# Output projection by tile groups with kept weight tiles, operand sums on VectorE, and one pool for merge and MLP

## The chip, the cores and the metric

The kernel runs on one core of a Trainium2 chip. The metric is the device time of one execution in microseconds. Before the change it is 1648.05 us, the median of three runs (1645.05, 1648.05 and 1648.10 us).

## The reference, cut to what matters

One layer of a decoder: two attention branches on the same normalized input, a gated merge, an output projection, and an MLP with squared ReLU. T = 1024 rows, D = 1024, DFF = 4096, everything in fp32. The change lies behind the attention branches, from `merged` on.

```python
def rms_norm(x, g):
    return x * rsqrt(mean(x * x, axis=-1) + 1e-6) * g

# o_fox, o_nsa [T, 512]: outputs of the attention branches; g_a, g_b [T, D]: columns of h @ w_in
merged = sigmoid(g_a) * (o_fox @ w_br_fox) + sigmoid(g_b) * (o_nsa @ w_br_nsa)
x = x + merged @ w_out                          # w_out [1024, 1024]
h = rms_norm(x, g_mlp)
x = x + square(relu(h @ w_ff1)) @ w_ff2         # w_ff1 [1024, 4096], w_ff2 [4096, 1024]
return rms_norm(x, g_final)
```

## The kernel before

**A product in fp32.** An operand is split into a high part, its cast to float32r ("hi", on ScalarE), and a low part, the operand less its high part ("lo", a subtraction). A product is three TensorE passes: lo x hi, hi x lo, hi x hi. All matmuls are issued on L157 and all transposes on L160, so the tile names tell them apart. A weight of the output projection is loaded into a buffer `wr` (2 of them), cast to `wh` (L205) and subtracted to `wl` (L206, VectorE); there are 3 buffers of each. The queue of a `w` load is SP's, as that of nearly all loads and stores; SP issues them in program order, and one that waits for a buffer holds those behind it.

**What is behind the attention.** `merge` computes the second branch product and keeps `merged`, transposed and split (its low part on L1394, VectorE), as `mrg[half] = (mh, ml)`, a half being 512 rows, that is four row tiles of 128. Then four pieces follow.

1. *w_out.* Its 1024 x 1024 weights are taken in eight blocks of 256 rows by 512 columns, 512 KB each. A block (u, ch) times a row tile i is six matmuls of 128 x 512, "a tile" below, accumulated in a psum bank `wo`. There are three groups: row tiles 0 to 3 (`wout0`, 2 x 16 tiles), row tiles 4 and 5, row tiles 6 and 7 (`wout1`, 16 tiles each). Every group loads and splits all eight blocks, 24 in all. When a row tile's column half is complete, `x1_done` adds the residual (L1441), and after the second half stores the row tile to DRAM (L1443), works out the RMS factor (L278 and L265 are small operations of it) and scales by it and by g_mlp (L1449).
2. *Turning.* The MLP needs h transposed. `turned` issues four 128 x 128 transposes into one of two psum banks (`psT`, tiles `tn_m`): "a turn". `first_half` (row tiles 0 to 3) casts it to hi (L1498, ScalarE), subtracts to lo (L1499, VectorE) and copies it to `bf` (L1506, ScalarE). `second_half` (row tiles 4 to 7) forms the sums that the scheme of the MLP needs, t1 to t4 (L1515, L1522, L1524 on VectorE or ScalarE, L1526 and L1529 on POOL), and splits each; two of the splits, and those of `rest`, go to POOL through the argument `eng`.
3. *w_ff1.* It is one level of a seven-product Strassen-Winograd scheme (`FIRST`), with operand sums on both sides. The 4096 columns are taken in 16 pairs u of two 128-column halves; `raw_half(u, x)` loads one half (512 KB, `r4`, four buffers), `wsum` forms the pair's weight sums on POOL (L1616 to L1619), `wsplit1` casts and splits the operands of one of four groups g (L1606, L1607; `w1h`, `w1l`). A product i of a pair is `ff1(u, i)`: three passes of four matmuls into bank X, W or Z. Products 0 and 1 need no sums. For three leading pairs (`LEADU`) they are issued ahead of the rest, between the last turns. `ff1_done` reads the banks, squares and stores hidden tiles to DRAM (`hid_d`); for the leading pairs this is put off (`defer`) until the pool `ff` opens in `hidden`, which does the rest of the scheme.
4. *w_ff2* in `output`: a second scheme of seven products, its weights loaded in quadrants of 8 KB per partition (pools `fo` and `f0`) and subtracted to their low parts on L1777 (VectorE, tiles `to`), and the final norm.

**What sets the order.** Python issues the instructions; the Tile scheduler orders them per engine by its estimates, dependences and the pools' buffers. `tc.issue_after(self.last.ins)` pins a TensorE step behind the one before. `placed(at, extra, steps)` puts the extra steps (the turns) at the places `at` among the numbered steps: a turn at 6.1 stands behind step 6. The tables `FFT1` and `FFT` are these places in the third group and among the leading products; the turns of the second group were spread evenly by `interleave`. A pool opened later than another gets its memory when the tiles there are released.

Of the kernel before, what the change touches and what calls it, by code (L numbers as in the profile page):

```python
# [18 lines left out]
P = 128  # L19
T = 1024  # L20
D = 1024
NT = 8
# [102 lines left out]
class Kernel:  # L125
# [1247 lines left out]
    def merge(self):  # L1373
# [6 lines left out]
        with tc.tile_pool(name="x1", bufs=8) as xp, tc.tile_pool(name="mg", bufs=3) as mp:  # L1380
            self.att = mp
            box = {}
            mrg = [None, None]
            st = Steps()

            def done(f, half, ps, sg):
                sg, pf = sg
                nc.vector.tensor_mul(sg, ps, sg)
                nc.vector.tensor_add(sg, sg, pf)
                if mrg[half] is None:  # L1390
                    mrg[half] = (hx_tile(f"mh{half}") if half else self.big_tile("mh0"), hx_tile(f"ml{half}"))
                th, tl = (t[:, f] for t in mrg[half])
                nc.scalar.copy(th, sg)
                nc.vector.tensor_sub(tl, sg, th.bitcast(F32))  # L1394

            def stage(f, half):

                if f < 2:
                    if not box:
                        box["t"] = self.big_tile("msn", F32)  # L1400
                    c = 4 * f + 2 * half
                    t = box["t"][:, c:c + 2]
                else:
                    t = xp.tile([P, 2, H], F32, tag="o", name=f"msn{f}{half}")
                for x, d in enumerate((self.gb_d, self.ga_d)):
                    nc.sync.dma_start(t[:, x], d[f * P:(f + 1) * P, half * H:(half + 1) * H])
                return t[:, 0], t[:, 1]

            self.branch(st, a["w_br_nsa"], stage, "n", lambda: self.on, done, True)
            self.commit(st)  # L1410
            wo = {}

            def wo_add(r, ch, u):
                wo[r, ch, u] = self.wadd([(None, a["w_out"][u * 256:u * 256 + 256, ch * H:ch * H + H].rearrange(
                    "(k p) c -> p k c", p=P))], f"wo{r}{ch}{u}", shape=(2, H), now=True)
# [21 lines left out]
            def x1_done(i, ch, acc):
                x = x1[i]
                th, j = divmod(i, 4)
                c = slice(ch * H, ch * H + H)  # L1440
                nc.vector.tensor_add(x[:, c], acc, x[:, c])  # L1441
                if ch == 1:
                    nc.sync.dma_start(self.x1_d[i * P:(i + 1) * P, :], x)  # L1443

                    junk = dest("t1" if th else "b11", j, self.big_tile, whole=True)
                    r = self.rstd(x.rearrange("p (a b) -> p a b", b=P), junk, f"m{i}")
                    for c in range(2):
                        cs = slice(c * H, c * H + H)
                        nc.vector.scalar_tensor_tensor(x[:, cs], x[:, cs], r, gm[:, cs], OP.mult, OP.mult)  # L1449
                    ys[th].append([x[:, 0:H], x[:, H:D]])  # L1450

            def wout0(ch):
                acc = [(self.psS if j < 2 else self.psP)(f"wo0{ch}{j}") for j in range(4)]

                def part(u, j):
                    wpart(acc[j], mrg[0], wo[0, ch, u], 2 * u, slice(j * P, j * P + P), u == 0, u == 3)
                    if u == 3:
                        x1_done(j, ch, acc[j])

                return [(6 * MM, lambda u=u, j=j: part(u, j)) for u in range(4) for j in range(4)]  # L1460

            def wout1(r):
                acc = {(ch, j): (self.psP if ch else self.psS)(f"wo1{r}{ch}{j}") for ch in range(2) for j in range(2)}

                def part(u, ch, j):
                    i = 2 * (r - 1) + j
                    wpart(acc[ch, j], mrg[1], wo[r, ch, u], 2 * u, slice(i * P, i * P + P), u == 0, u == 3)
                    if u == 3:
                        x1_done(4 + i, ch, acc[ch, j])

                return [(6 * MM, lambda u=u, ch=ch, j=j: part(u, ch, j))
                        for u in range(4) for ch in range(2) for j in range(2)]

            gm = mp.tile([P, D], F32, tag="gm", bufs=1, name="g_mlp_b")
            nc.sync.dma_start(gm, ap(a["g_mlp"], 0, [[0, P], [1, D]]))
            for i in range(NT):
                xt = xp.tile([P, D], F32, tag="o", name=f"x1_{i}")
                nc.sync.dma_start(xt, a["x"][i * P:(i + 1) * P, :])
                x1.append(xt)


            V = self.hv = {}

            def turned(y, c, name):
                pt = self.psT(f"tn_{name}_{c}")
                for k in range(4):
                    self.tr(pt[:, k * P:(k + 1) * P], y[c][:, k * P:(k + 1) * P], self.idn)
                return pt.rearrange("p (k t) -> p k t", k=4)

            def dest(key, j, alloc, whole=False):  # L1490
                if key not in V:
                    V[key] = alloc(f"h{key}")
                t = V[key][:, :, j * P:(j + 1) * P]
                return t if whole else (t[:, 0:4], t[:, 4:8])

            def split(key, j, src, alloc, eng, full=None):
                hi, lo = dest(key, j, alloc)
                nc.scalar.copy(hi, src)  # L1498
                eng.tensor_sub(lo, src if full is None else full, hi.bitcast(F32))  # L1499

            def first_half(j, c):
                pv = turned(ys[0][j], c, f"m0{j}")
                split("b21" if c else "b11", j, pv, self.big_tile, nc.vector)
                if c == 0:
                    bf.append(xp.tile([P, 8, P], F32, tag="o", name=f"bf{j}"))
                nc.scalar.copy(bf[j][:, 4 * c:4 * c + 4, :], pv)  # L1506
# [55 lines left out]
            for f in rest:  # L1562
                f()
# [388 lines left out]
```

## Time and profile before

| | |
|---|---|
| median of three runs | 1648.05 us |
| profiled execution, its own time | 1649.16 us |
| its span (first to last instruction) | 1647.5 us |
| granted TensorE clock, mean over the span | 0.984 |
| busy, share of the span | PE 97%, PE's weight load 82%, VectorE (DVE) 67%, ScalarE (ACT) 52%, GpSimd (POOL) 25% |
| DMA queues | 37.7% of 16 engines' span |

In the rows below, PE is a matmul or transpose, PEld its weight load, L157 a line of the kernel. A row of the list of groups gives line, engine, operation, output<-inputs, shapes and count, then the busy time and the mean in ns of one, then the engine's idle time just ahead of them and what ended it. A row of the list of waits gives the waiting group, what released it, the total in us, the count and the longest. A row of the chain gives when a piece began and how long it was. A row of stretches has the window in us from the span's start, its length, the busy time of PE, PEld, DVE, ACT and POOL, each with its count, then the granted clock (1.00 is full speed), the share of the DMA engines and GB/s.

### The profile page before, as it was taken

Reading aid. Unit: us, or ns where it says so; the run is one execution under the profiler, and the core shown is the slowest. Engines: PE = TensorE matmul, PEld = TensorE weight load, DVE = VectorE, ACT = ScalarE, POOL = GpSimd, SP = SyncE. Lnnn points to the kernel's source line nnn. Section 1 sums busy time; section 2 is a strip of 40 time slices with the busy share of each in tenths; the row PEclk is TensorE's granted clock in tenths of the full one; section 3 lists DMA queues with packets and bytes.
Section 4 is the critical chain, followed back from the end, with each engine's and each line's share of the span. In section 5 each row is a group of like instructions: output and inputs, shape, how many; then the busy total and the mean of one; then the engine's idle time right before and its main releaser. Section 6 shows DMA issues by size and latency. Waiting matters only on the chain.

```text
span 1647.5 us, 23820 instructions
## 1 busy us (share of the span) xinstructions
PE 1596.6 (97%) x8245; PEld 1351.1 (82%) x8245; DVE 1102.1 (67%) x2339; ACT 861.2 (52%) x1636; POOL 416.6 (25%) x486
## 2 busy tenths in 40 slices
PE   6999999999999999999999998799999999999997
PEld 5788888888888888898988876688888878888886
DVE  8556666765655675576767479565566579787876
ACT  4456566645555565567553265555555544333334
POOL 7122122212333322346330007433333200000004
PEclk7999999999999999999999998899999999999999
DMA  5321211342222212124348561454444597444412
GB/s 171 59 68 35 60 61 35 111 113 62 69 56 64 65 38 73 53 65 140 126 150 273 196 216 63 148 175 144 157 146 152 183 326 245 150 136 155 135 52 102
DMA packets 166080, 198.79 MB, mean 121 GB/s; under 512 B 21112, under 2 KB 100792, under 8 KB 165952
## 3 DMA queue, kind: packets, MB, share of 16 engines
q1 hardware_dynamic: 165960, 197.27, 37.7%
q8 instruction: 65, 1.06, 0.3%
q14 instruction: 55, 0.45, 0.1%
HBM read 142.09 MB, written 55.15 MB: 120 GB/s over the span
## 4 chain that ended last, share of the span: by engine, by line
PE 86%; DVE 6%; DMA 4%; issue 2%; ACT 2%; POOL 1%; SPq 0%; ACTq 0%; DVEq 0%; POOLq 0%
PE g L157 11%; PE fX L157 10%; PE accs L157 8%; PE oX L157 8%; PE fZ L157 5%; PE oZ L157 4%; PE ptn L160 4%; PE fq L157 3%; PE nq L157 3%; PE fv L157 3%; PE brf L157 3%; PE wo L157 3%; PE fk L157 3%; PE sf L157 2%; PE brn L157 2%; PE fW L157 2%
## 5 line engine op out<-in xcount | busy, mean ns | idle before, releaser
L157 PE MATMUL oX<-to,so 128*128 128x512 f32 x672 | 155.3, 390 | 1.9 <-DVE to L1777 1.3
L157 PEld LDWEIGHTS oX<-to,so 128*128 128x128 f32 x672 | 125.9, 188 | 29.2 <-DVE to L1777 1.7
L1776 ACT CAST to<-w 128x1024 fp32r<-128x1024 f32 x48 | 48.1, 1051 | 143.9 <-PE accs L157 53.2
L820 DVE TENSOR_TENSOR PTn<-ptn,PTn 128x512 fp32r<-128x512 f32 (+2 forms) x136 | 82.0, 610 | 52.0 <-ACT PTn L819 51.4
L819 ACT CAST PTn<-ptn 128x512 fp32r<-128x512 f32 (+2 forms) x136 | 69.3, 521 | 55.5 <-PE ptn L160 49.4
L1892 POOL TENSOR_TENSOR z<-x,gf 128x512 f32<-128x512 f32 x14 | 18.9, 1369 | 310.9 <-DVE x L1825 307.5
L157 PE MATMUL fX<-ht,w1h 128*128 128x512 f32 x384 | 95.8, 392 | 0.0
L796 POOL TENSOR_SCALAR pf<-pf,rdf 128x896 f32<-128x896 f32 (+3 forms) x64 | 47.4, 748 | 178.7 <-DVE rdf L795 154.0
L157 PE MATMUL accs<-PTn,Vnv 128*128 128x256 f32 x480 | 91.0, 305 | 0.0
L157 PEld LDWEIGHTS fX<-ht,w1h 128*128 128x128 f32 x384 | 72.9, 190 | 15.4
L1607 DVE TENSOR_TENSOR w1l<-w,w1h 128x1024 fp32r<-128x1024 f32 (+1 forms) x32 | 37.6, 1174 | 65.4 <-ACT w1h L1606 65.3
L157 PE MATMUL g<-hTl,wh_g 128*128 128x512 f32 (+1 forms) x280 | 78.0, 399 | 0.0
L157 PE MATMUL oZ<-to,so 128*128 128x512 f32 x336 | 77.5, 389 | 0.0
L157 PEld LDWEIGHTS accs<-PTn,Vnv 128*128 128x128 f32 x480 | 72.2, 189 | 2.7 <-DVE otn L829 0.4
L157 PEld LDWEIGHTS oZ<-to,so 128*128 128x128 f32 x336 | 63.1, 188 | 13.1
L157 PE MATMUL g<-hTh,wh_g 128*128 128x512 f32 (+1 forms) x280 | 73.2, 389 | 0.0
L157 PE MATMUL g<-hTh,wl_g 128*128 128x512 f32 x256 | 72.2, 400 | 0.0
L1777 DVE TENSOR_TENSOR so<-hr,so 128x1024 fp32r<-128x1024 f32 x56 | 68.3, 1240 | 2.6 <-ACT so L1776 2.5
L1776 ACT CAST so<-hr 128x1024 fp32r<-128x1024 f32 x56 | 56.5, 1049 | 17.7 <-DMA hr<-hid_d 17.7
L1616 POOL TENSOR_TENSOR ss<-w 128x512 f32<-128x512 f32 x16 | 26.2, 1639 | 144.6 <-DVE w1l L1607 136.8
L1777 DVE TENSOR_TENSOR to<-w,to 128x1024 fp32r<-128x1024 f32 x48 | 56.7, 1223 | 7.7 <-ACT to L1776 7.7
L157 PE MATMUL fX<-ht,w1l 128*128 128x512 f32 x192 | 52.4, 395 | 9.5 <-ACT h L1680 8.8
(521 smaller groups left out, 4393.8 us busy)
## 6 DMA issues: line engine op xcount, KB each, us to landing
hr<-hid_d SPq DMA_DIRECT2D x56, 512.0 KB, 4.9
w<-in_w_ff_dram SPq DMA_DIRECT2D x32, 512.0 KB, 4.6
hid_d<-s SPq DMA_DIRECT2D x64, 256.0 KB, 2.0
w<-in_w_ff_dram SPq DMA_DIRECT2D x15, 1024.0 KB, 5.7
wr_wo<-in_w_out_dram SPq DMA_DIRECT2D x24, 512.0 KB, 4.5
hid_d<-h SPq DMA_DIRECT2D x48, 256.0 KB, 2.9
x<-in_x_dram SPq DMA_DIRECT2D x16, 512.0 KB, 7.1
wr_g<-in_w_in_dram SPq DMA_DIRECT2D x16, 512.0 KB, 3.9
```

Source lines behind the costliest of these rows:

```text
L157: self.last = self.nc.tensor.matmul(*a, **k)
L160: self.last = self.nc.tensor.transpose(*a, **k)
L796: nc.gpsimd.tensor_scalar(p, p, r, 1.0 if gate is None else gate, op0=OP.mult, op1=OP.mult)
L819: nc.scalar.copy(th, src)
L820: nc.vector.tensor_sub(tl, src, th.bitcast(F32))
L1607: nc.vector.tensor_sub(lo, src, hi.bitcast(F32))
L1616: e.tensor_add(p[:, 4:8], b[:, 0:4], b[:, 4:8])
L1776: nc.scalar.copy(o[:, 0, s], src)
L1777: nc.vector.tensor_sub(o[:, 1, s], src, o[:, 0, s].bitcast(F32))
L1892: nc.gpsimd.tensor_mul(y[:, c], x[:, c], gf[:, c])
```

## The change

- w_out goes by the row tile groups (0, 1, 4, 5), (2, 3) and (6, 7). Inside a group the order of blocks is written out (`WO`) so that the first two blocks of the second and third group are the last two of the group before: their split tiles are kept (`wo[r, u, ch] = wo[r - 1, u, ch]`) and not loaded again. 20 blocks are loaded.
- Row tiles 0, 1, 4, 5 are done first, so turns of both halves stand in the second group (table `AT1`, one turn after each of six tiles), and first-half turns of tiles 2 and 3 in the third (`AT2`).
- All sums and splits of `second_half` and `rest` are on VectorE, and `wsum` of pair 0 too; t3 and t4 are formed in place.
- One pool `o4` of 4 KB tiles (8 under tag "o", 2 under tag "p") serves x1, the buffers of the turns, the hidden tiles of w_ff1 and the weights of w_ff2, which are therefore loaded in half quadrants. The pools `x1`, `mg`, `ff`, `f0` and `fo` are gone; the leading pairs' `ff1_done` follow straight behind the leading products.
- There are four leading pairs. The fourth pair's first half is loaded behind the last turn of `AT3`; its banks are `psT`, which the turns have left.

```diff
-        with tc.tile_pool(name="x1", bufs=8) as xp, tc.tile_pool(name="mg", bufs=3) as mp:
+        xp = self.o4 = self.ctx.enter_context(tc.tile_pool(name="o4", bufs=8))
...
-            for ch in range(2):
-                for u in range(4):
-                    wo_add(0, ch, u)
-            for r in (1, 2):
-                for u in range(4):
-                    for ch in range(2):
-                        wo_add(r, ch, u)
+        for r, blocks in enumerate(self.WO):
+            for n, (u, ch) in enumerate(blocks):
+                if r and n < 2:
+                    wo[r, u, ch] = wo[r - 1, u, ch]
+                    continue
+                wo[r, u, ch] = self.wadd(...)
...
+        gm = xp.tile([P, D], F32, tag="p", bufs=2, name="g_mlp_b")
+        odd = xp.tile([P, 2, H], F32, tag="p", bufs=2, name="odd")
...
-            def split(key, j, src, alloc, eng, full=None):
+        def split(key, j, src, alloc):
                 hi, lo = dest(key, j, alloc)
                 nc.scalar.copy(hi, src)
-                eng.tensor_sub(lo, src if full is None else full, hi.bitcast(F32))
+            nc.vector.tensor_sub(lo, src, hi.bitcast(F32))
...
+        def second_half(j, c):
+            pv = turned(ys[4 + j], c, f"m{4 + j}")
+            t1 = q(odd[:, j % 2])
+            if c == 0:
+                nc.vector.tensor_sub(t1, pv, bf[j][:, 0:4, :])
+                split("t1", j, t1, self.big_tile)
+                return
+            two = xp.tile([P, 2, H], F32, tag="o", name=f"bt_{j}")
+            b22, t2 = q(two[:, 0]), q(two[:, 1])
+            nc.scalar.copy(b22, pv)
+            nc.vector.tensor_sub(t2, pv, t1)
+            split("t2", j, t2, self.big_tile)
+            nc.vector.tensor_sub(t1, t2, bf[j][:, 0:4, :])
+            split("t3", j, t1, hx_tile)
+            nc.vector.tensor_sub(t2, bf[j][:, 4:8, :], t2)
+            rest.append(lambda: (split("b22", j, b22, hx_tile), split("t4", j, t2, hx_tile)))
...
-            run(wout0(0))
-            run(wout0(1))
-            w1 = wout1(1)
-            run(w1[:4] + interleave(turns(range(4), first_half), w1[4:]))
+        run(wout(0))
+        placed(self.AT1, turn(first_half, (0, 0), (0, 1), (1, 0), (1, 1)) + turn(second_half, (0, 0), (1, 0)), wout(1))
         self.ff1_prepare()
...
-            placed(self.FFT1, turns((0, 1), second_half), w2[:12])
+        placed(self.AT2, turn(second_half, (0, 1), (1, 1)) + turn(first_half, (2, 0), (2, 1), (3, 0), (3, 1)) +
+               none(lambda: self.wsplit1(0, 0), lambda: self.wsplit1(1, 0)), wout(2))
...
-            placed(self.FFT, turns((2, 3), second_half), lead)
-            self.wsum(0)
-            for f in rest:
-                f()
+        placed(self.AT3, turn(second_half, (2, 0), (2, 1), (3, 0), (3, 1)) +
+               none(lambda: (self.wsum(0), self.raw_half(3, 0))), lead)
+        self.wsplit1(0, 1)
+        done, self.defer = self.defer, None
+        for u in range(self.LEADU):
+            done[u, 0]()
+        for u in range(self.LEADU):
+            done[u, 1]()
+            rest[u]()
-    FFT1 = (6.1, 7.1, 9.1, 10.1)
-    FFT = (4.1, 5.1, 8.1, 9.1)
-    LEADU = 3
+    WOT = (0, 1, 4, 5), (2, 3), (6, 7)
+    WO = ([(u, ch) for ch in range(2) for u in range(4)],
+          [(3, 1), (2, 1), (3, 0), (2, 0), (1, 1), (1, 0), (0, 0), (0, 1)],
+          [(0, 1), (0, 0), (1, 0), (1, 1), (2, 0), (2, 1), (3, 0), (3, 1)])
+    AT1 = (6.1, 7.1, 8.1, 9.1, 10.1, 11.1)
+    AT2 = (1.1, 3.1, 8.1, 9.1, 11.1, 12.1, 11.2, 13.2)
+    AT3 = (12.1, 13.1, 15.1, 16.1, 13.2)
+    LEADU = 4
...
-            e = self.nc.gpsimd
+            e = self.nc.gpsimd if u else self.nc.vector
...
-                U[bank] = (self.psS if bank == "X" else self.psX if (u, i) == (2, 1) else self.psP)(f"f{bank}{u}{i}")
+                alloc = {(2, 1): self.psX, (3, 0): self.psT, (3, 1): self.psT}
+                U[bank] = alloc.get((u, i), self.psS if bank == "X" else self.psP)(f"f{bank}{u}{i}")
...
-                t = pool.tile([P, G, H], F32, tag=tag, name=f"{k}_{c}")
-                nc.sync.dma_start(t, quadrant(c, k))
+                for q in range(G // 2):
+                    tag, b = ("p", 2) if k == "w12" else ("o", 8)
+                    t = self.o4.tile([P, 2, H], F32, tag=tag, bufs=b, name=f"{k}_{c}{q}")
+                    nc.sync.dma_start(t, quadrant(c, k)[:, 2 * q:2 * q + 2])
```

The order of instructions at three places, before and after. The number behind a tile's name is its own, so two rows with one number are the same tile.

*TensorE in the second group, where the first turns stand.* `wo` rows are w_out, x2 two matmuls; `tn_m_0` and `tn_m_1` are the two column halves of a turned row tile. Before:

```order
L157 MATMUL wo_10944<-wl_wo_11020,mh_10304 128x512 x2
L157 MATMUL wo_10944<-wh_wo_11019,mh_10304 128x512 x2
L160 MATMUL tn_m_0_11031<-idn,x_1_10608 128x128 x4
L160 MATMUL tn_m_1_11058<-idn,x_1_10608 128x128 x4
L157 MATMUL wo_10945<-wl_wo_11047,mh_10304 128x512 x2
L157 MATMUL wo_10945<-wh_wo_11046,mh_10304 128x512 x2
```

and after:

```order
L160 MATMUL tn_m_0_11000<-idn,x_0_10604 128x128 x4
L157 MATMUL wo_10981<-wh_wo_10969,ml_10281 128x512 x2
L157 MATMUL wo_10981<-wl_wo_10970,mh_10280 128x512 x2
L157 MATMUL wo_10981<-wh_wo_10969,mh_10280 128x512 x2
L160 MATMUL tn_m_1_11015<-idn,x_0_10604 128x128 x4
L157 MATMUL wo_10942<-wh_wo_10988,ml_10281 128x512 x2
L157 MATMUL wo_10942<-wl_wo_10989,mh_10280 128x512 x2
L157 MATMUL wo_10942<-wh_wo_10988,mh_10280 128x512 x2
L160 MATMUL tn_m_0_11036<-idn,x_1_10606 128x128 x4
```

Before, two turns stand together and more tiles lie between such couples; now a turn stands after each tile, six times.

*ScalarE at the same place*, which casts both weight blocks (L205) and turned tiles (L1498 before, L1492 after) and copies the latter to `bf` (L1506 before, L1500 after), upon which their bank is free. Before:

```order
L205 CAST wh_wo_11019<-wr_wo_10969 128x1024
L1498 CAST hb_10858<-tn_m_0_10983 128x4x128
L1498 CAST hb_11015<-tn_m_1_11010 128x4x128
L205 CAST wh_wo_11046<-wr_wo_10996 128x1024
L1506 COPY bf_10990<-tn_m_0_10983 128x512
L1506 COPY bf_10990<-tn_m_1_11010 128x512
```

and after:

```order
L1492 CAST hb_10856<-tn_m_0_11000 128x4x128
L205 CAST wh_wo_11059<-wr_wo_10992 128x1024
L1492 CAST hb_11020<-tn_m_1_11015 128x4x128
L1500 COPY bf_11007<-tn_m_0_11000 128x512
L1492 CAST hb_10856<-tn_m_0_11036 128x4x128
L1500 COPY bf_11007<-tn_m_1_11015 128x512
L205 CAST wh_wo_11093<-wr_wo_11028 128x1024
```

Both now and before one weight cast stands between a bank's cast and the copy that frees it; now it stands ahead of the second turn's cast too, and the next weight cast behind two turns that are a tile apart.

*SP's queue at the start of the MLP.* `w_11`, `w_21`, `w_30` are halves of the w_ff1 pairs 1, 2 and 3, `w_0` (before) and `w_00` (after) a part of w_ff2, `x_d` rows store row tiles, `hid_d` rows store hidden tiles. Before:

```order
L186 DMA wr_wo_11313<-in_w_out_dram 128x2x512
L1588 DMA w_11_11633<-in_w_ff_dram 128x8x128
L1443 DMA x_d<-x_6_10618 128x1024
L1443 DMA x_d<-x_7_10620 128x1024
L1588 DMA w_21_11674<-in_w_ff_dram 128x8x128
```

and after:

```order
L1586 DMA w_30_11501<-in_w_ff_dram 128x8x128
L1439 DMA x_d<-x_6_10616 128x1024
L1439 DMA x_d<-x_7_10618 128x1024
L1747 DMA w_00_13752<-in_w_ff_dram 128x2x512
L1670 DMA hid_d<-h11h_0_11575 128x512
L1670 DMA hid_d<-h11h_1_11577 128x512
L1670 DMA hid_d<-h11h_2_11579 128x512
L1586 DMA w_11_11625<-in_w_ff_dram 128x8x128
```

Pair 1's second half `w_11` stood ahead of the last row tiles' stores and of all hidden stores; now the first half of pair 3 stands ahead of those stores, and `w_11` behind three hidden stores.

On POOL all rows of L1526, L1529 and L1499 and pair 0's four rows of L1616 to L1619, which stood first in this part of the program, are gone; its first rows are now the weight sums of pairs 1 and 2.

More of the change, by code (lines that the diff above doesn't have):

```diff
@@ new lines, in stage @@
+        def stage(f, half):
+            if f < 2:
+                if not box:
+                    box["t"] = self.big_tile("msn", F32)
+                c = 4 * f + 2 * half
+                t = box["t"][:, c:c + 2]
+            else:
+                t = xp.tile([P, 2, H], F32, tag="o", name=f"msn{f}{half}")
+            for x, d in enumerate((self.gb_d, self.ga_d)):
+                nc.sync.dma_start(t[:, x], d[f * P:(f + 1) * P, half * H:(half + 1) * H])
+            return t[:, 0], t[:, 1]
@@ new lines, in merge @@
+        self.branch(st, a["w_br_nsa"], stage, "n", lambda: self.on, done, True)
+        self.commit(st)
+        wo = {}
+        for r, blocks in enumerate(self.WO):
[3 more added lines that the diff above has]
+                    continue
+                wo[r, u, ch] = self.wadd([(None, a["w_out"][u * 256:u * 256 + 256, ch * H:ch * H + H].rearrange(
+                    "(k p) c -> p k c", p=P))], f"wo{r}{ch}{u}", shape=(2, H), now=True)
@@ new lines, in wout, with part @@
+        def wout(r):
+            tiles = self.WOT[r]
+            blocks = self.WO[r]
+            acc = {}
+            def part(n, i):
+                u, ch = blocks[n]
+                mine = [x for x in range(8) if blocks[x][1] == ch]
+                first, last = n == mine[0], n == mine[-1]
+                if first:
+                    wide = (i < 2, ch == 1, ch == 0)[r]
+                    acc[ch, i] = (self.psS if wide else self.psP)(f"wo{r}{ch}{i}")
+                th, j = divmod(i, 4)
+                wpart(acc[ch, i], mrg[th], wo[r, u, ch], 2 * u, slice(j * P, j * P + P), first, last)
+                if last:
+                    x1_done(i, ch, acc[ch, i])
+            return [(6 * MM, lambda n=n, i=i: part(n, i)) for n in range(8) for i in tiles]
@@ new lines, in merge, with placed @@
+        rest = []
+        def placed(at, extra, steps):
+            for n, (c, f) in sorted([*zip(at, extra), *enumerate(steps)], key=lambda x: x[0]):
+                if c:
+                    with tc.issue_after(self.last.ins), tc.high_priority(offset=0 if n == int(n) else self.TP):
+                        f()
+                else:
+                    f()
+        turn = lambda f, *jc: [(4 * TR, lambda j=j, c=c: f(j, c)) for j, c in jc]
+        none = lambda *fs: [(0, f) for f in fs]
+        run(wout(0))
@@ L1840, in tail @@
             if not tb:
[L1841 to L1842 removed]
+                tb["j"], tb["y"] = (self.o4.tile([P, D], F32, tag="o", name=f"tail{x}") for x in range(2))
             y = tb["y"]
```

283 lines of the change are left out of this document (103 added, 180 removed).

## The prediction

> **What bounds the kernel now.** I read the page first, then busy time by stretches, then the waits and the chain inside the one stretch that is not full.
>
> ```profile
> span 1647.5 us, 23820 instructions
> PE 1596.6 (97%) x8245; PEld 1351.1 (82%) x8245; DVE 1102.1 (67%) x2339; ACT 861.2 (52%) x1636; POOL 416.6 (25%) x486
> PEclk7999999999999999999999998899999999999999
> ...
> core 0: us, PE busy (x) PEld busy (x) DVE busy (x) ACT busy (x) POOL busy (x), PEclk, DMA share, GB/s
> 905.00:998.00 93.00, 90.94 (x420) 73.70 (x418) 61.13 (x100) 46.31 (x68) 6.09 (x4) 1.00 0.58 197
> 998.00:1006.00 8.00, 4.44 (x12) 3.22 (x13) 8.00 (x7) 3.27 (x6) 7.92 (x6) 0.74 0.00 0
> 1006.00:1029.00 23.00, 20.50 (x86) 16.52 (x85) 22.31 (x31) 12.39 (x21) 17.42 (x11) 0.87 0.19 68
> 1029.00:1040.00 11.00, 2.21 (x8) 1.48 (x8) 5.45 (x5) 3.50 (x7) 8.06 (x6) 0.66 0.40 103
> 1040.00:1330.00 290.00, 289.27 (x1271) 239.02 (x1270) 174.80 (x175) 161.63 (x236) 92.26 (x56) 1.00 0.50 167
> 1330.00:1636.00 306.00, 304.09 (x1344) 251.11 (x1343) 239.79 (x282) 116.67 (x133) 17.46 (x13) 1.00 0.46 155
> ```
>
> TensorE is the bound everywhere but in 998 to 1040, where it works 27.15 of 42 us, VectorE is full, and the granted clock falls: the end of the w_out product, the four leading steps' transposes, and the start of the MLP. The waits between 940 and 1045, and the chain through it:
>
> ```profile
> PE fX L157 <- ACT h L1680: 8.8, 1, 8.8
> PE wo L157 <- DVE wl_wo L206: 4.5, 2, 3.5
> PE tn_m L160 <- issue: 2.5, 1, 2.5
> ...
> 904.80 38.09 PE wo L157 x168
> ...
> 960.69 3.61 DMA wr_wo<-in_w_out_dram
> 964.40 1.06 ACT wh_wo L205
> 965.48 1.24 DVE wl_wo L206
> 966.73 3.79 DMA wr_wo<-in_w_out_dram
> ...
> 999.29 0.60 DVE t L1524
> 999.88 0.60 DVE x L1441
> ...
> 1038.90 4.83 PE fX L157 x12
> 1043.73 2.74 PE fZ L157 x12
> ```
>
> One 128x512 matmul at full clock takes 38.09 / 168 = 0.227 us. From 904.80 to 1043.73 (138.9 us) TensorE issues 384 of w_out, 84 of the MLP and 16 turns of four transposes. A turn's cost is the step between these two rows:
>
> ```profile
> 990.66 0.60 PE L160 MATMUL tn_m<-idn,x 128*128 128x128 f32 x4
> 991.01 0.71 PE L157 MATMUL wo<-wh_wo,ml 128*128 128x512 f32 x2
> ```
>
> So 468 x 0.227 + 16 x 0.35 = 111.7 us of work, and **27.2 us are lost** there. That is all the change can win in this stretch. Of it 15.8 us are the three waits above. Part of the rest is clock: behind the wait of 2.5 us (1012.2 to 1014.7) the next microseconds read
>
> ```profile
> 1015.00:1016.00 1.00, 1.00 (x6) 0.85 (x5) 1.00 (x3) 0.00 (x0) 0.00 (x0) 0.76 0.00 0
> 1016.00:1017.00 1.00, 1.00 (x5) 0.70 (x5) 1.00 (x2) 0.21 (x1) 0.00 (x0) 0.50 0.00 0
> ...
> 1019.00:1020.00 1.00, 1.00 (x6) 0.79 (x5) 1.00 (x2) 0.49 (x1) 1.00 (x1) 1.00 0.00 0
> ```
>
> that is between 3 and 4 us at half clock, about 1.7 us lost. The other wl_wo wait (4.5 - 3.5 = 1.0 us) lies in 905 to 998, whose clock stays 1.00. So a wait of 1.0 us keeps the clock and one of 2.5 us lost it.
>
> **The change, part by part.** The engines' prices:
>
> ```profile
> L206 DVE TENSOR_TENSOR wl_wo<-wr_wo,wh_wo 128x1024 fp32r<-128x1024 f32 x22 | 28.5, 1295 | 25.2 <-ACT wh_wo L205 25.2
> L1499 DVE TENSOR_TENSOR ht<-t,ht 128x512 fp32r<-128x512 f32 x8 | 12.5, 1570 | 0.0
> L1499 DVE TENSOR_TENSOR hb<-tn_m,hb 128x512 fp32r<-128x512 f32 x8 | 5.3, 682 | 0.0
> L1394 DVE TENSOR_TENSOR ml<-msn,mh 128x512 fp32r<-128x512 f32 x4 | 2.6, 689 | 0.0
> L1449 DVE SCALAR_TENSOR_TENSOR x<-x,r_m,g_mlp_b 128x512 f32<-128x512 f32 x16 | 11.1, 749 | 0.1
> L278 DVE TENSOR_SCALAR t_m<-t_m 128x1 f32<-128x1 f32 x8 | 1.1, 149 | 0.0
> L1499 POOL TENSOR_TENSOR ht<-t,ht 128x512 fp32r<-128x512 f32 x4 | 7.0, 1755 | 0.0
> L205 ACT CAST wh_wo<-wr_wo 128x1024 fp32r<-128x1024 f32 x22 | 23.1, 1049 | 40.4 <-DMA wr_wo<-in_w_out_dram 22.3 <-PE wo L157 18.0
> L1506 ACT COPY bf<-tn_m 128x512 f32<-128x512 f32 x8 | 4.6, 586 | 0.3 <-DVE hb L1499 0.2
> ...
> wr_wo<-in_w_out_dram SPq DMA_DIRECT2D x24, 512.0 KB, 4.5
> ```
>
> *Sums on VectorE alone, and no pool change.* The same subtraction of SBUF operands takes 0.69 us (L1394, POOL idle) and 1.57 us (L1499 ht, POOL at work). Back to back such an operation holds VectorE 0.60 (the two 0.60 pieces of the chain), 0.09 less than it lasts; a split of 1024 columns by the same 0.09 holds it 1.15. The change takes 20 POOL operations out of the stretch (16 of the pairs' sums and splits, 4 of the first weight sum) and puts them on VectorE at 0.60 = 12 us; with POOL quiet the eight slowed splits of the L1499 ht row alone get back 12.5 - 8 x 0.69 = 7 us, and the weight splits beside them a few more. The 8.8 us wait ends behind POOL's last splits and behind a pool that opens only then; with one pool for both stages, ScalarE's copies of the leading pairs wait for TensorE alone. That wait goes. What is late next is VectorE.
>
> *VectorE's total.* From the end of the first group to the first product that needs the last sums: 74 operations of 512 columns x 0.60, 16 of them (L1449) 0.06 dearer, 17 splits of 1024 x 1.15, 40 small ones (L278) x 0.1: 69 us. TensorE has 16 blocks x 2.72 + 8 leading products x 2.72 + 16 turns x 0.35 = 70.9. VectorE fits with 2 us to spare, so each wait of its own past that shows up. Followed operation by operation through the third group and the leading pairs, it comes out 1.0 us late for the last weight block and level with TensorE at the end. I charge 1.0 + 0.5, ends 0 and 6 (a quarter of the 25.2 us for which it waits at L206 now).
>
> *Groups and kept tiles.* 20 weight blocks are loaded and split, not 24: four 512 KB loads, four casts (4 x 1.05) and four subtractions (4 x 1.15) fewer. In the second and third group two blocks of eight need no weights. Supply: load 3.7, cast 1.06, subtraction 1.24, two buffers: 3.0 us a block, against 2.72 + 0.35 of TensorE; the two free blocks (5.4 us) cover it. So weights don't stop TensorE by themselves.
>
> *Turns closer together.* Six turns now stand one tile (1.36 us) apart. Each needs one of two psum banks, which comes free after ScalarE's cast, VectorE's split and ScalarE's copy, and between these stand weight casts that wait for loads. With t = 0 at the second group's start: the cast of weight block (1,1) needs the buffer of the second kept block, free at 5.44, and ends at 6.5; VectorE comes to it from block (2,0) at 7.2 and is done at 8.35. The load behind it lands at 12.45 (4.1, between the chain's 3.7 and the page's 4.5), its cast ends at 13.5, then ScalarE's cast of the second turn (0.6) at 14.1 and the copy that frees the first bank at 14.7. TensorE wants the bank after 9 tiles and two turns, 12.9: it waits 1.8 us. The same chain one block on: 1.6 us. Sum 3.4, ends 2.6 and 4.8 by the load's time, plus one loss of clock, 1.7 (ends 0 and 3.4).
>
> *Four leading pairs.* Neutral in work. The fourth pair's first half takes the load buffer that pair 1's second half had, so that load now waits until pair 0's last split, and on SP's queue behind three stores of hidden tiles. After the last turn ScalarE has 16 operations x 0.58 (as L1506) + 1.05 = 10.3 us before the third tile is squared, while TensorE has 28 matmuls left, 6.35: the third store can go 4.0 us after the leading pairs. Then the load, three POOL sums, cast 1.05 and subtraction 1.15:
>
> ```profile
> w<-in_w_ff_dram SPq DMA_DIRECT2D x32, 512.0 KB, 4.6
> ...
> L1616 POOL TENSOR_TENSOR ss<-w 128x512 f32<-128x512 f32 x14 | 22.8, 1629 | 143.4 <-DVE w1l L1607 136.8 <-DMA w<-in_w_ff_dram 6.6
> ```
>
> 4.0 + 4.6 + 3 x 1.63 + 2.2 = 15.7 us after the leading pairs, where TensorE arrives after five products, 13.6. A new wait of 2.1 us (ends 0 and 4), and a clock loss of 1.7 (0 to 1.7). Pair 2's sums have 13.6 us more and come in time.
>
> *Output stage.* Its first w_ff2 tiles wait now until all stores of the last pair are out; the one wait of TensorE behind them is
>
> ```profile
> 1359.14 4.37 PE L157 MATMUL oX<-to,so 128*128 128x512 f32 x18 [1.27 <-DVE to L1777]
> ```
>
> With 4 KB tiles they are issued between those stores. I take 0.5 us of 1.27. Twice as many loads at half the size cost nothing where TensorE is busy 304 of 306 us.
>
> *Sum.* Left lost: 3.4 + 1.7 + 1.5 + 2.1 + 1.7 = 10.4, and about 1.5 us of small gaps that 27.2 contains today and that stay (my estimate: TensorE stands idle for about as much, 93.00 - 90.94 = 2.1 us, in 905 to 998): 11.9. Gain 27.2 - 11.9 + 0.5 = 15.8 us. The profiled execution took 1649.16 us (span 1647.5), the median of the runs is 1648.05, 1.1 below it. 1649.2 - 15.8 = 1633.4, on the median's scale **1632**.
>
> The trace has a wait of 2.5 us that lost the clock. The Trainium skill ("TensorE: Matmul & The Clock Gate", Part 1 and "HAM oscillation") puts the limit at idle gaps of about 3.4 us of a free-running window. By that rule the new waits, 1.6 to 2.1 us, would mostly keep the clock; the trace agrees only in part, since 2.50 us was enough once.
>
> **The rivals.**
> - *The clock holds* through all new waits: speaks for it that 1.0 us left it alone, against it the 2.5. Then 3.4 us less are lost: 1629. (The rule of the Trainium skill's page above would end here.)
> - *VectorE becomes the bound.* It must work 69 of 71 us, and the 25.2 us of waits at L206 show that it stands behind loads. If a third of these come back in the second and third group, 8 us: 1640. For it: both are in-order queues with weight splits ahead of what frees the banks. Against: two blocks in eight need no weights.
> - *The VectorE price is its own* and not POOL's doing: slower. If SBUF subtractions cost 1.57 alone, 29 of them would add 0.97 x 29 = 28 us, less the 2 to spare: 1658. It decides from 0.6 us more per operation on. Against it stand 689 ns of L1394 and 682 of L1499 hb.
> - *The change moves the stall, no more*: each of pairs 1 to 3 waits for its late half, which adds 2 x (2.1 + 1.7) = 7.6, and banks and VectorE cost their upper ends (4.8 + 3.4 + 6): 27 us lost again, 1647. Against: one load's delay is paid once.
>
> **How the numbers follow.** The sum as worked out 0.56, the clock 0.15, VectorE 0.20, the price 0.04, the moved stall 0.05. No change is within 0.2% (3.3 us), about what a measurement here can tell. Faster: 0.91, of which I keep 0.90; same 0.05; slower 0.05. All low ends of the sum together are 7.8 us fewer lost (1624), all high ones 9.5 more (1642); they don't all fall together, and half of each, 1628 to 1637, is the first case's own range. The whole range goes on to most of VectorE's case and of the clock's: 1626 to 1643.
>
> **What the profile after would show.** TensorE's wait for ScalarE's h gone; L1493, L1517 and L1520 at 0.69 us with POOL empty until the MLP's sums; short TensorE waits at the turns of the second group and none over 3 us; one of 2 to 3 us before pair 1's third product, released by VectorE's w1l; clock dips only there. Wrong it is if VectorE waits for casts in the third group, or if the wait before pair 1 is over 6 us.

## The result

The changed kernel takes 1629.74 us (median of four runs, 1628.83 to 1630.91), the kernel before 1648.07 us; the ratio is 0.9891, 95% interval 0.9874 to 0.9908. That is 18.3 us less; 15.8 us less was forecast. The profiled execution took 1629.54 us.

The page of the changed kernel, its first lines:

```profile
span 1627.5 us, 23814 instructions
PE 1590.8 (98%) x8245; PEld 1348.5 (83%) x8245; DVE 1095.3 (67%) x2355; ACT 855.6 (53%) x1632; POOL 381.3 (23%) x466
...
PEclk7999999999999999999999999999999999999999
```

The two 8s in the middle of the clock's row are gone, and the span is 20.0 us shorter with as many matmuls. The stretches that answer to those shown of before (columns as there: length, PE, PEld, DVE, ACT, POOL, clock, DMA share, GB/s):

```profile
904.00:997.00 93.00, 89.88 (x410) 73.78 (x408) 61.00 (x106) 42.41 (x63) 0.00 (x0) 0.98 0.51 177
997.00:1005.00 8.00, 7.78 (x37) 6.51 (x37) 8.00 (x12) 6.27 (x11) 0.00 (x0) 1.00 0.38 125
1005.00:1020.00 15.00, 15.00 (x76) 12.45 (x74) 13.00 (x28) 7.68 (x15) 0.00 (x0) 1.00 0.20 73
1020.00:1026.00 6.00, 6.00 (x28) 4.98 (x27) 6.00 (x10) 6.00 (x12) 0.00 (x0) 1.00 0.01 3
```

From 997 on TensorE works nearly without a gap; the one place with a lower clock has moved to the second group. All of TensorE's waits between 900 and 1060, and where they stand in time (start, length, the idle time ahead and what ended it):

```profile
PE tn_m L160 <- ACT bf L1500: 3.3, 2, 3.0
PE fX L157 <- DVE w1l L1605: 1.6, 1, 1.6
```

```profile
963.65 0.66 PE L160 MATMUL tn_m<-idn,x 128*128 128x128 f32 x4 [3.00 <-ACT bf L1500]
997.22 0.66 PE L160 MATMUL tn_m<-idn,x 128*128 128x128 f32 x4 [0.34 <-ACT bf L1500]
1041.09 1.21 PE L157 MATMUL fX<-ht,w1l 128*128 128x512 f32 x4 [1.56 <-DVE w1l L1605]
```

So the 8.8, 4.5 and 2.5 us of before are gone, and the two new waits are those that the prediction named: the third turn of the second group waits for its bank, and pair 1's third product for its late second half. ScalarE's rows show the chain of the first:

```profile
961.58 1.04 ACT L205 CAST wh_wo<-wr_wo 128x1024 fp32r<-128x1024 f32 x1 [1.15 <-DVE wl_wo L206]
962.53 0.58 ACT L1492 CAST hb<-tn_m 128x512 fp32r<-128x512 f32 x1
963.00 0.59 ACT L1500 COPY bf<-tn_m 128x512 f32<-128x512 f32 x1
```

The copy that frees the bank stands behind a weight cast that begins only at 961.58, and the turn goes 0.06 us after the copy's end. VectorE's groups between 940 and 1034 (busy us, mean ns):

```profile
L206 DVE TENSOR_TENSOR wl_wo<-wr_wo,wh_wo 128x1024 fp32r<-128x1024 f32 x11 | 13.4, 1222 | 5.0 <-ACT wh_wo L205 5.0
...
L1493 DVE TENSOR_TENSOR ht<-odd,ht 128x512 fp32r<-128x512 f32 x8 | 5.5, 688 | 0.7 <-ACT ht L1492 0.7
...
L1517 DVE TENSOR_TENSOR odd<-bt,bf 128x512 f32<-128x512 f32 x4 | 2.8, 690 | 0.0
```

688 ns where the split of SBUF operands took 1570.

### The profile page after: what moved, and what is told of

Same layout as the page of the kernel before. It is cut to its first block, busy times and chain, and to the rows that moved or that the text cites. A ratio compares the mean times of both kernels' runs of the same rounds, so it can differ in the third digit from the quotient of the medians.

```text
span 1627.5 us, 23814 instructions
## 1 busy us (share of the span) xinstructions
PE 1590.8 (98%) x8245; PEld 1348.5 (83%) x8245; DVE 1095.3 (67%) x2355; ACT 855.6 (53%) x1632; POOL 381.3 (23%) x466
## 5 line engine op out<-in xcount | busy, mean ns | idle before, releaser
L157 PEld LDWEIGHTS oZ<-to,so 128*128 128x128 f32 x336 | 63.1, 188 | 13.1
L793 ACT ACTIVATE pf<-pf,mf 128x896 f32<-128x896 f32 (+3 forms) x64 | 49.5, 774 | 20.4 <-DVE mf L780 17.5
```

The costliest lines, as they stand in the source:

```text
L157: self.last = self.nc.tensor.matmul(*a, **k)
L793: nc.scalar.activation(p, p, AF.Exp, bias=nm, scale=-1.0, accum_out=den)
```

## The experiments

All times are medians of four runs, each beside runs of the kernel before. Before w_out starts, all these kernels run the same instructions, yet the first w_out matmul stands anywhere from 901.1 to 905.2 us in the fourteen profiles. The clock goes with it: half clock comes in pieces of 3.41 us (last section), and w_out begins at 901.1 to 901.5 in the four profiles with four or five such pieces ahead of it, at 902.4 to 905.2 in the ten with six to eight; whether that is the cause is not shown. So beside the time I give the *stretch*: from the first w_out matmul to the first w_ff2 matmul of the profiled execution, which leaves that scatter out. It is still that of one execution, in which a piece of half clock more or less is worth about 1.7 us, so differences below 2 us in it are not put down to an edit by themselves. What follows it, to the span's end, takes 316.8 and 317.3 us with the old pools (first run, and before) and 314.9 to 315.4 us in every kernel with the one pool.

| kernel | time, us | ratio to before, 95% | stretch, us |
|---|---|---|---|
| before | 1648.07 | | 425.6 |
| changed | 1629.74 | 0.9874 to 0.9908 | 408.3 |
| 1. before, sums on VectorE | 1642.03 | 0.9947 to 0.9977 | 418.8 |
| 2. changed, sums on POOL | 1635.44 | 0.9906 to 0.9940 | 414.0 |
| 3. changed, turns two tiles apart | 1627.51 | 0.9857 to 0.9886 | 405.7 |
| 4. changed, early second half of pair 1 | 1626.18 | 0.9850 to 0.9879 | 405.3 |
| 5. old groups, 24 blocks, 3 pairs, one pool | 1635.79 | 0.9911 to 0.9939 | 416.8 |
| 6. changed, no kept tiles | 1629.59 | 0.9869 to 0.9903 | 408.9 |
| 7. changed, 3 leading pairs | 1633.83 | 0.9891 to 0.9924 | 413.2 |
| 8. edits 3 and 4 together | 1625.77 | 0.9841 to 0.9870 | 404.1 |
| 9. changed, old groups | 1627.66 | 0.9860 to 0.9896 | 407.4 |
| 10. as 8, turns three tiles apart | 1625.01 | 0.9847 to 0.9881 | 404.0 |
| 11. as 5, 4 pairs and late turns | 1631.64 | 0.9892 to 0.9925 | 411.3 |
| 12. as 5, late turns | 1640.25 | 0.9943 to 0.9973 | 419.2 |

**1. The sums on VectorE, in the kernel before.** In `second_half`, `rest` and `wsum`:

```diff
-nc.gpsimd.tensor_sub(t2, b22, t1)
+nc.vector.tensor_sub(t2, b22, t1)
...
-e = self.nc.gpsimd
+e = self.nc.gpsimd if u else self.nc.vector
```

> The kernel before with one part of the change alone: the 16 sums and splits of second_half and rest and pair 0's four weight sums go from POOL to VectorE; groups, pools and leading pairs stay. Theory (the last wait before the third product, 8.8 us, is set by POOL's late splits, and VectorE's splits are slowed by POOL beside them): the splits on L1499 come down from 1.57 to 0.7 us, the 8.8 us wait falls to 3 to 6 us (the pool opening still stands behind the last splits), time 1642 to 1646. Rival (the pool that opens late is the whole of the wait): the wait stays at 8 us or more and the time within 2 us of the kernel before. Second rival (VectorE, full in this stretch, becomes the bound by 12 us more work): slower than the kernel before, 1650 or more.

Its longest waits between 900 and 1060, and the rows of VectorE and ScalarE at the end of the first:

```profile
PE fX L157 <- ACT h L1680: 4.3, 1, 4.3
PE wo L157 <- DVE wl_wo L206: 3.8, 2, 3.1
PE tn_m L160 <- issue: 2.5, 1, 2.5
...
```

```profile
1030.82 0.68 DVE L1499 TENSOR_TENSOR ht<-bt,ht 128x512 fp32r<-128x512 f32 x1
```

```profile
1031.53 1.57 ACT L1680 COPY h<-fX 128x512 f32<-128x512 f32 x3 [1.19 <-DVE ht L1499]
```

6.5 us faster, 6.8 in the stretch: VectorE has twenty operations more (sixteen sums and splits, four weight sums) and is done sooner, at 1031.50 in place of 1033.44 us. The wait fell from 8.8 to 4.3 us, so both rivals are out. Some 5.1 of the 6.8 us are clock: the stretch has three pieces of half clock where before has six. What is left of it ends when VectorE's last split is done (1031.50) and the leading pairs' copies begin 0.03 us later.

**2. The same part undone in the changed kernel**: the splits of t2 and t4, the sums of t4 and pair 0's weight sums are issued on `nc.gpsimd`, 16 of the 20 operations (the sums of t2 stay on VectorE).

> The changed kernel with that part undone: the splits of t2, the sums of t4 and the splits of t4 (12 operations) and pair 0's four weight sums go back to POOL. Theory: POOL needs 16 x 1.6 = 26 us for them and VectorE's operations beside them go from 0.69 to 1.5 us, so the third product of pair 0 waits for a split again, by 4 to 10 us, and the clock falls: 1636 to 1644. Rival (the groups and the one pool give the gain, POOL's share is hidden behind the fourth leading pair): within 2 us of the changed kernel, 1628 to 1632.

5.7 us more in the time as in the stretch, 0.6 us below the range expected. TensorE's longest waits, and VectorE's groups between 975 and 1045:

```profile
PE tn_m L160 <- ACT bf L1500: 4.2, 2, 3.1
PE fX L157 <- DVE w1l L1605: 2.9, 1, 2.9
PE fX L157 <- POOL ht L1493: 1.7, 1, 1.7
...
```

```profile
L206 DVE TENSOR_TENSOR wl_wo<-wr_wo,wh_wo 128x1024 fp32r<-128x1024 f32 x5 | 9.3, 1868 | 2.1 <-ACT wh_wo L205 2.1
...
L1517 DVE TENSOR_TENSOR odd<-bt,bf 128x512 f32<-128x512 f32 x4 | 4.9, 1234 | 0.0
...
L1515 DVE TENSOR_TENSOR bt<-tn_m,odd 128x512 f32<-128x512 f32 x4 | 2.7, 683 | 0.4 <-ACT bt L1514 0.4
```

Pair 0's third product does wait for a split of POOL's, but by 1.7 us and not by the 4 to 10 expected; the rest of the loss is the longer waits at the banks and before pair 1's third product (2.9 us, with a piece of half clock behind it). The same instructions take 1868 in place of 1222 ns, and 1234 in place of 690, with POOL at work. L1515, whose first operand lies in psum, keeps its 683 ns; so does L1499 `hb<-tn_m` in the kernel before (682). The Trainium skill ("SBUF — State Buffer", "Who interferes with whom") says just this: a VectorE instruction with two SBUF inputs contends with a GpSimd one that reads SBUF, and one with at most one SBUF input, some modes aside, does not. These rows agree.

**3. The turns two tiles apart.**

```diff
-    AT1 = (6.1, 7.1, 8.1, 9.1, 10.1, 11.1)
+    AT1 = (6.1, 7.1, 9.1, 10.1, 12.1, 13.1)
```

> The changed kernel with the table AT1 = (6.1, 7.1, 9.1, 10.1, 12.1, 13.1) in place of (6.1, 7.1, 8.1, 9.1, 10.1, 11.1): couples of turns with a free tile between. Theory (TensorE's 3.0 us wait for the bank that ScalarE's copy frees stands in the chain weight load, cast, copy, whose end the place of the turn doesn't move): the third turn comes 1.36 us later, so the wait falls to about 1.6 us, which keeps the clock; 1.4 + 1.7 = 3.1 us less, 1626 to 1627.5. Rival (the chain moves with the turns, as the later turns' own casts delay the next weight casts): the wait turns up at a later turn, time within 1 us of 1629.7.

```profile
PE tn_m L160 <- ACT bf L1500: 2.7, 3, 1.4
PE fX L157 <- DVE w1l L1605: 1.5, 1, 1.5
```

The wait of 3.00 became one of 1.41 and, later, one of 0.98; the clock is 1.00 throughout the stretch. 2.6 us less there: 0.6 of waiting at the banks and 1.7 of clock are 2.3 of it. Both theories had a part: the first wait shrank by the place of the turn, and about 1 us came back at a later one.

**4. Pair 1's second half early.**

```diff
-none(lambda: (self.wsum(0), self.raw_half(3, 0)))
+none(lambda: (self.wsum(0), self.raw_half(3, 0), self.wsplit1(0, 3), self.raw_half(1, 1)))
```

> The changed kernel with pair 0's last weight split and then the load of pair 1's second half issued right behind the load of pair 3's first half, so ahead of the hidden tiles' stores in the queue. Theory (the 1.6 us wait before pair 1's third product is the late load): the load goes out before 1020 instead of at 1029.5, the wait is gone, 1.6 us less, 1628. Rival (the split tiles' three buffers are the limit: a tile held early makes pair 0's own splits late): a new wait of 1 to 4 us before the third or fifth product of pair 0, time 1629 to 1633.

```profile
963.12 0.65 PE L160 MATMUL tn_m<-idn,x 128*128 128x128 f32 x4 [2.51 <-ACT bf L1500]
...
1030.22 1.15 PE L157 MATMUL fX<-ht,w1l 128*128 128x512 f32 x4 [0.43 <-DVE w1l L1605]
```

```profile
1007.29 0.38 SPq L1586 DMA_DIRECT2D w<-in_w_ff_dram  x1
```

The load goes out at 1007.3 in place of 1029.5, the 1.6 us wait is gone, and pair 0's own fifth product now waits 0.43 us for its split: the theory, with a trace of the rival. The stretch is 3.0 us shorter, more than the 1.2 us that this explains; the rest is that the bank wait, 2.51 us here, left the clock at 1.00 in this execution (why, the last section shows).

**5. The one pool with the old order.** Old groups, no kept tiles, three pairs, turns at the old places:

```diff
-    WOT = (0, 1, 4, 5), (2, 3), (6, 7)
+    WOT = (0, 1, 2, 3), (4, 5), (6, 7)
...
-                if r and n < 2:
+                if False:
...
-    AT3 = (12.1, 13.1, 15.1, 16.1, 13.2)
-    LEADU = 4
+    AT3 = (4.1, 5.1, 8.1, 9.1, 17.2)
+    LEADU = 3
```

> The changed kernel with the old groups (row tiles 0 to 3, 4 and 5, 6 and 7), all 24 weight blocks loaded and three leading pairs: of the change only the one pool and the sums on VectorE are left, so beside the first run it tells what the one pool is worth. Theory (in the first run the 4.3 us wait ends 0.7 us after VectorE's last split, because the leading pairs' copies wait for a pool that opens only then): the copies start as soon as TensorE is done, the wait falls to 1 us or less and the clock loss behind it with it: 1642 less 4 to 6, 1636 to 1638. Rival (the third product waits for VectorE's last sums themselves, the pool opening only coincides): a wait of 2.5 us or more released by VectorE's split, 1639 to 1642.

```profile
PE tn_m L160 <- issue: 4.2, 1, 4.2
PE wo L157 <- DVE wl_wo L206: 3.0, 1, 3.0
...
PE fX L157 <- DVE ht L1493: 0.4, 1, 0.4
```

The wait for ScalarE's copies fell from 4.3 to 0.4 us, as the theory says, and the rival's wait of 2.5 us is not there. But the wait for a row tile's scaling ahead of its turn grew from 2.5 to 4.2 us (its row says only `issue`; VectorE's scaling L1445 began at 1011.37, the turn at 1012.23), and the stretch is shorter by 2.0 us alone, with three pieces of half clock in both. Of the 6.6 us between the spans of the two profiles only these 2.0 and the 1.6 us behind the stretch can be put down to the pool and what comes with it (t3 and t4 formed in place, w_ff2 in half quadrants); in the other 3.0 us w_out began sooner, which no edit of this kernel touches. The times differ by 6.2 us, of which the share of that scatter is not known.

**6. No kept tiles** (`if False:` in place of `if r and n < 2:`).

> The changed kernel with all 24 weight blocks of w_out loaded, cast and subtracted: no tile is kept between groups. Theory (a block costs 3.0 us of supply against 2.7 to 3.1 us of TensorE; the free blocks pay for the turns' work on ScalarE and VectorE): TensorE waits for weights or for the turns' banks by 2 to 6 us more in the second and third group, one more clock loss, 1632 to 1638. Rival (supply has room, the wait is that of the turns alone): 1629 to 1631.

```profile
961.27 0.66 PE L160 MATMUL tn_m<-idn,x 128*128 128x128 f32 x4 [1.65 <-ACT bf L1500]
966.82 0.66 PE L160 MATMUL tn_m<-idn,x 128*128 128x128 f32 x4 [1.67 <-ACT bf L1500]
```

The rival was right: no difference. There is 0.8 us more of waiting at the banks and 0.6 us at a row tile's scaling, and no wait for a weight; but no wait is over 1.7 us and the clock stays, where the changed kernel lost 1.7 us behind its 3.00 us wait.

**7. Three leading pairs** (`LEADU = 3`, the load of pair 3's half taken out of `AT3`).

> The changed kernel with three leading pairs in place of four; pair 3's first half is loaded where it was before. Theory (the fourth pair covers VectorE's last sums): TensorE comes to pair 0's third product 5.4 us earlier and waits 3 to 5 us for VectorE's splits or ScalarE's copies, with a clock loss; the 1.6 us wait before pair 1 goes, since its load has its buffer back: 1631 to 1635. Rival (VectorE is not the limit there): 1627 to 1629, the wait before pair 1 gone and nothing in its place.

```profile
PE fX L157 <- ACT ht L1492: 5.1, 1, 5.1
PE tn_m L160 <- ACT bf L1500: 3.0, 2, 2.7
...
```

As the theory says: 5.1 us before the third product, the clock falls there, the wait before pair 1 is gone. The row names a cast of ScalarE's; VectorE works beside it with no gap over 0.1 us from 1011.8 to 1030. 4.9 us more in the stretch.

**9. The old groups in the changed kernel**: `WOT` as in the fifth run, all first-half turns in the second group.

> The changed kernel with the old row groups (0 to 3, 4 and 5, 6 and 7); kept tiles, one pool, VectorE's sums and four leading pairs stay. All turns of the second group are then first halves, at 4.1, 5.1, 7.1, 8.1, 10.1, 11.1, 13.1, 14.1; four second-half turns stand in the third group and four among the leading products. Theory (with the sums of two row tiles done a group earlier, VectorE has less to do at the end): VectorE's sums crowd into the last 40 us, TensorE waits 2 to 5 us for a split or a bank there, 1631 to 1635. Rival (four leading pairs are cover enough, the order of row tiles is worth nothing): 1628 to 1630.5.

My theory was wrong, and the time is even 0.3 us below the rival's range: 1627.66 us, a stretch of 407.4. The four pairs are cover enough whichever row tiles come first; the longest wait at a bank is 1.8 us.

**11 and 12. What is left when both go, and the turns alone.** The eleventh kernel is the fifth with four pairs and the last turns late, so it has old groups *and* 24 blocks; the twelfth is the fifth with the late turns alone (`AT3 = (12.1, 13.1, 15.1, 16.1, 17.2)`, three pairs).

> The kernel of the fifth run (old groups, 24 weight blocks, one pool, VectorE's sums) with the fourth leading pair and the last turns behind 12 leading steps, as in the changed kernel. So the kept tiles and the new groups are both left out of the changed kernel. Measured as the stretch from the first w_out matmul to the first w_ff2 matmul, which was 416.8 us in the fifth run and 408.4 in the changed kernel. Theory (the fourth pair, with the room it gives the last turns, is the whole of that difference): 407 to 410 us, the waits of 4.2 us at a turn and 3.0 us at a weight gone, time 1627 to 1631. Rival (kept tiles and new groups each replace the other, but one of the two is needed): a weight wait of 2 us or more with a clock loss, 411 to 414 us, 1631 to 1635.

> The kernel of the fifth run with one edit: the last four turns stand behind 12 of the 18 leading steps in place of 4; still three leading pairs. Theory (the late turns need the fourth pair behind them): the 4.2 us wait at a turn goes, and a wait of 4 to 6 us before pair 0's third product takes its place: stretch 414 to 418 us, time 1633 to 1637. Rival (the turns' place alone is the gain): no wait over 2 us, 409 to 412 us, 1629 to 1632.

The eleventh's waits:

```profile
PE wo L157 <- DVE wl_wo L206: 2.9, 1, 2.9
PE tn_m L160 <- ACT bf L1500: 2.3, 2, 1.4
PE fX L157 <- DVE w1l L1604: 1.4, 1, 1.4
...
```

and the twelfth's:

```profile
PE fX L157 <- ACT ht L1492: 3.8, 1, 3.8
...
PE fX L157 <- DVE ht L1493: 2.5, 1, 2.5
...
```

The eleventh fell to the rival: with neither kept tiles nor new groups a weight wait of 2.9 us is back, and the clock falls behind it. With one of the two alone nothing of it is left (run 6) or 1.1 us that keeps the clock (run 9), so undoing one shows nothing. The twelfth came out slower than I gave it: late turns without the fourth pair are 2.4 us worse in the stretch than early ones, with 6.3 us of waits at the third product.

**8 and 10. A faster version.** Edits 3 and 4 together, and then `AT1 = (6.1, 7.1, 10.1, 11.1, 13.1, 14.1)`.

> The changed kernel with both edits: turns two tiles apart, and the early load of pair 1's second half. Theory: both saved waits add, but each run alone already kept the clock after the bank wait, which can be kept only once: 1629.7 less 1.6 less 2.2, 1625 to 1626.5. Rival (the early load's own gain of 3.5 us was a load that happened to land sooner in the second group, the turns' spacing adds nothing): 1626 to 1628.

> The kernel with both edits, and the turns of the second group moved on: AT1 = (6.1, 7.1, 10.1, 11.1, 13.1, 14.1), the third turn three tiles behind the second. Theory (the bank wait ends at a time set by the weight load): the third turn's 1.2 us go, the later turns' waits stay or fall to about 1 us together: 1624.5 to 1625.5. Rival (the waits move on to the later turns and to the third group's first turn): 1625.5 to 1627.

The waits of the eighth:

```profile
PE tn_m L160 <- ACT bf L1500: 2.3, 3, 1.2
PE fX L157 <- DVE w1l L1605: 0.4, 1, 0.4
```

1625.77 and 1625.01 us: the eighth's interval lies wholly below the changed kernel's, the tenth's overlaps its lower end; in the stretch they are 4.2 and 4.3 us shorter. The two cannot be told apart: in the tenth the third turn's wait fell from 1.2 to 0.3 us and the fifth's rose from 0.8 to 1.4, so the rival of the tenth is right about the place of the wait.

## Why the prediction was right, and where its terms were off

Right: the sign, the time within 2.3 us, the kind and place of the waits that go and of those that come. In its own terms, from the first w_out matmul to pair 1's third product: 1041.09 - 903.77 = 137.3 us, with (384 + 156) x 0.2267 + 16 x 0.35 = 128.0 us of work, so 9.3 us lost where 11.9 were forecast.

| term | forecast left, us | measured, us |
|---|---|---|
| turns waiting for a bank | 3.4 | 3.3 |
| clock behind it | 1.7 | 1.7 |
| VectorE late | 1.5 | 0 |
| pair 1's late second half | 2.1 | 1.6 |
| clock behind it | 1.7 | 0 |
| small gaps | 1.5 | 2.7 (the rest) |
| gain of the output stage | 0.5 | 1.9 |

- *Bank waits.* The sum is right, its parts are not: 1.8 + 1.6 were forecast, 3.0 + 0.3 came; that they add up alike is luck. The weight cast in the chain began at 961.58, 14.3 us after the second group's start (the first group takes 32 tiles, 43.5 us, from 903.77), where I had its load land at 12.45 us: VectorE's subtraction freed the load's buffer at 956.30, 9.0 us after the start and not 8.35, and from there to the cast it took 5.3 us and not 4.1.
- *Clock.* A slice of 1 us with a clock of 0.85 has 0.3 us at half clock, one of 0.50 (there are three) the whole, one of 0.95 has 0.1: the slices below make 3.4 us at half clock behind the 3.00 us wait, half of it lost: 1.7. That term came out by luck: it was charged to a wait of 1.8 us, and no wait that short lost the clock in this part of any of the profiles. The wait of 1.56 us kept the clock. Charging it there too was the step that failed most: I knew that 1.0 us kept the clock and 2.5 lost it, and put 2.1 with the latter.

```profile
964.00:965.00 1.00, 1.00 (x7) 0.82 (x6) 0.52 (x2) 0.66 (x2) 0.00 (x0) 0.85 0.33 125
965.00:966.00 1.00, 1.00 (x4) 0.81 (x3) 0.65 (x1) 0.41 (x1) 0.00 (x0) 0.50 0.54 178
...
968.00:969.00 1.00, 1.00 (x6) 0.80 (x5) 1.00 (x2) 0.52 (x2) 0.00 (x0) 0.95 0.00 0
```

- *VectorE.* It fits, as worked out, and was never late in the third group or behind the leading pairs. That it has little to spare is shown by run 7: 5.4 us less of cover brought a wait of 5.1 us. The rival in which VectorE becomes the bound was one leading pair away.
- *The price of a sum.* The rival that 1.57 us is VectorE's own price is refuted twice: 688 ns here, and the same lines slower again with POOL at work in run 2.
- *The 8.8 us wait.* The prediction took it as one thing that goes with the sums and the pool together. Runs 1 and 5 split it: the sums on VectorE took 4.5 us of it, the pool that opens late 3.9. It also read VectorE as full from 998 to 1040; in its own row from 1029 on VectorE works 5.45 of 11 us, and from 1033.44 it stood idle behind POOL's last splits, which end at 1038.23.
- *Output stage.* 0.5 us of a 1.27 us wait were counted. That wait and another of 0.6 us for `x` on L1825 are gone, and the stage is 317.3 - 315.4 = 1.9 us shorter; 1.9 to 2.4 us it is in every kernel with the one pool (1.4 to 1.9 beside the first run).
- *Rest of w_ff1.* Not in the sum: one wait on L1677 grew from 0.7 to 1.3 us (`h22s`), and in all some 0.9 us more are lost from pair 1 on. The rival in which pairs 2 and 3 wait for their late halves as well did not come: this is TensorE's only wait behind pair 1's in w_ff1.

Added up on the span: 27.2 - 9.3 = 17.9 gained up to pair 1, 0.9 lost behind it, 1.9 gained in the output stage, and w_out began 0.9 us sooner by scatter: 19.8 of the 20.0 us.

Part by part, by the stretch: the sums 425.6 to 418.8 (6.8 us); the one pool to 416.8 (2.0, and 1.6 behind the stretch); the fourth pair together with late turns to 411.3 (5.5); kept tiles or new groups to 408.3 (3.0), one of them being enough. Late turns alone lose 2.4 us (run 12) and the changed kernel without the fourth pair 4.9 (run 7); the fourth pair with early turns was not run. Clock is about 5.1 us of the first of these steps and 3.4 of the third (pieces of half clock in the stretch: 6, 3, 3, 1, 1). The prediction called the fourth pair neutral and charged it only with its new wait; with the late turns it carries about a third of the gain, as the cover without which VectorE's sums would not fit. That the sum did come out near is owed to this: it was worked out with the cover in place.

## What to carry to other kernels

Read an operation's price with its neighbour: the same VectorE instruction cost 0.69 or 1.6 us by what POOL did beside it, and moving POOL's work *onto* the fuller engine made both sooner done. Ask of each part of a change what cover it gives, not only what it costs: undone alone, kept tiles and groups each looked worthless, yet leaving out both cost 3 us. And where a copy that frees a bank stands behind a cast that waits for a load, move the consumer by a tile or two before anything else.

## What the runs showed of the hardware that I had not expected

The half clock comes in pieces of one length: 3.4 us in the changed kernel, and in the kernel before two and three times as long, 6.9 and 10.3 us, from these rows (a clock of 0.57 over 8 us is 2 x 0.43 x 8 us at half clock, 0.53 over 11 us is 2 x 0.47 x 11):

```profile
1001.00:1009.00 8.00, 6.22 (x15) 4.93 (x16) 8.00 (x7) 4.27 (x8) 7.92 (x5) 0.57 0.01 2
1032.00:1043.00 11.00, 4.10 (x10) 3.26 (x11) 3.33 (x4) 5.30 (x10) 6.23 (x5) 0.53 0.67 202
```

It also begins with a delay: TensorE stands idle from 960.65 to 963.65, and the clock falls at about 964.7, when TensorE is at work again. A wait of 2.5 us cost the clock in the kernel before and 2.51 us did not in run 4; 1.8 us never did in the part from 895 to 1070 us.

The traces show what decides. Within one execution all pieces of half clock begin on one grid of 3.413 us; in the kernel before those at 1001.86, 1015.51 and 1032.58 are four and five steps apart. Cut into windows on that grid, the changed kernel (first two rows) and run 4 (last two) read:

```profile
961.28:964.69 3.41, 1.04 (x7) 0.97 (x8) 2.35 (x3) 2.37 (x4) 0.00 (x0) 1.00 0.46 156
964.69:968.11 3.42, 3.42 (x12) 2.75 (x11) 1.22 (x2) 2.33 (x5) 0.00 (x0) 0.50 0.42 153
958.54:961.96 3.42, 2.07 (x12) 1.38 (x9) 1.82 (x2) 2.44 (x3) 0.00 (x0) 1.00 0.40 142
961.96:965.37 3.41, 2.25 (x15) 1.87 (x15) 2.52 (x3) 2.30 (x6) 0.00 (x0) 1.00 0.61 163
```

In the changed kernel most of the wait lies in one window, TensorE works 1.04 us of it, and the next window has half clock. In run 4 the edge of a window halves the wait of 2.51 us, TensorE works over 2 us of each, and the clock stays. So it is in all fourteen profiles between 895 and 1070 us: each of the 16 windows at full clock in which TensorE worked 1.42 us or less was followed by half clock, none of the 678 in which it worked 1.75 us or more. (Over the whole executions the border lies between 1.55 and 1.69 us of idle time in a window, about half of it.) So a wait of 2 to 3 us costs 1.7 us or nothing by where it falls on the grid. No run sets the grid's place, and it differs from one execution to the next, so this part of a time is chance; the kernels of runs 3, 8 and 10, whose waits here are all under 1.5 us, are safe from it by these traces.

The Trainium skill ("TensorE: Matmul & The Clock Gate", Part 1) describes an activity window of about 3.4 us that runs free of the kernel's start. The lengths and the grid agree with it. Its limit, one idle window, does not: in the changed kernel the window ahead of the fall holds 1.04 us of TensorE's work.
